# RWKV's keys and receptances projected by blocks: seven products in place of eight

## The chip, the cores and the metric

The kernel runs on one core of one Trainium2 chip. The metric is the device time of one launch in microseconds (us); the profiler's record of one execution gives durations, waits and order. TensorE is PE (its weight loads PEld), VectorE DVE, ScalarE ACT, GpSimdE POOL; SyncE (SP) issues the DMA transfers.

## The reference

One layer over 512 tokens of width 1024, in fp32: a normalization, an input projection, two mixers side by side (a sparse attention, NSA, and RWKV-7), an output projection and an FFN. What the change touches is the projection of RWKV's receptances r and keys k:

```python
proj = rmsnorm(x, ln_mix_g[l]) @ w_in[l]              # (512 x 1024) @ (1024 x 3096)
y_rwkv = rwkv7_mixer(proj[..., NSA_COLS:], ...)
# in rwkv7_mixer:
prev = jnp.pad(cols, ((0, 0), (1, 0), (0, 0)))[:, :-1]
z = cols + (prev - cols) * mu
r, k, v, xw, xa, xg = jnp.split(z, ...)               # 512, 512, 512, 64, 64, 128 columns
kk = k * k_k;  kk = kk * rsqrt(max(sum(kk * kk), 1e-24))
```

## The kernel before

Each fp32 operand of a large product is split into a high part (a cast to fp32r, on ACT) and a low part (the difference, on DVE). A product of two such operands is three matmuls: high by high, high by low, low by high (`mm3`, L331 to 334). Tokens come in four tiles of 128. `norm_T` normalizes a tile, transposes it on PE and leaves its parts in XH and XL, two tensors each for the lower and upper 512 of the 1024 inputs.

The stage `rw_in` (L466) projects five blocks of 256 RWKV features with `feat_cols` (L443). The first holds decay, rate and gate (WA, SG) and runs in two halves of the tokens, since tiles 2 and 3 are normalized while it runs; then two blocks of keys and two of receptances. For a block PE runs over 8 parts of 128 inputs, 2 halves of 128 features and 3 matmuls, 48 in all, of 512 token columns. The weights come in quarters of 128x512, fetched four ahead, split three ahead (`piece`, L428). A block collects in two PSUM banks of one pair (`pa` or `pb`, in turn). When it is done, `shift_mix` (L392) mixes each feature row with the token before: ACT scales the shifted row (`sh`), DVE adds (L398). For the keys ACT squares and PE sums over columns (`pss`, L493); POOL takes a power (`rsk`). WA and SG are such mixes too.

All other streams (values, preparation, scan, attention) wait until `rw_in` sets `rw_kr` (L510). Streams are merged by priority and by a clock of estimated costs (the numbers that each `yield` returns), and a scheduler below that orders each engine's queue; each engine then works its queue in that order. SP's queue carries all loads, and each new load also waits for the one eight before it.

The FFN (L1279 to 1377) already uses seven products: `pair_blocks` for 12 of 16 blocks, `pair_direct` for the first of each half. Its differences of tokens are TT, made in `norms` (L1215 to 1225) in `traw` tiles, its weight sums are `ws`, its products `pw`, the partial sums `wu` and `cc`.

Of the kernel before, what the change touches and what calls it, by code (L numbers as in the profile page):

```python
# [9 lines left out]
F32 = mybir.dt.float32  # L10
# [7 lines left out]
T = 512  # L18
# [5 lines left out]
NT = 4  # L24
RU = 20
RA = 4
# [22 lines left out]
LS = 4  # L49
FV = 10  # L50
UNITS = [(i, g) for g in range(2) for i in range(NT)]
KD = 8
NSA = 1304
RW0 = 1304
# [60 lines left out]
def layer(ctx: ExitStack, tc: tile.TileContext, A, cst, out):  # L115
# [276 lines left out]
    def shift_mix(pa, m, outs):  # L392
# [4 lines left out]
        for i, o_ in enumerate(outs):  # L397
# [6 lines left out]
    COLS.update({f'v{b}': (RW0 + 1024 + 256 * b, 256, True) for b in range(2)})  # L404
    BLOCKS = [(RW0 + 6 * 256, 256, False), (RW0 + 512, 256, False), (RW0 + 768, 256, False), (RW0, 256, False),
              (RW0 + 256, 256, False)] + [COLS[n] for n in ORD]

# [19 lines left out]

    def piece(c0, h):  # L428

        while len(ahead) < 3 and pos_[0] < len(PIECES):  # L430
            p_ = pos_[0]
            c_, n, perm, h_ = PIECES[p_]
            f_ = p_ < 4
            ahead.append((c_, h_, wload(None, 2, n, perm, cycle('zv') if f_ else None, cycle('zr') if f_ else None,
                                        raw_piece(p_), G if f_ and FG else V)))
            for m_ in range(p_ + 1, min(p_ + 1 + RA, RU)):
                raw_piece(m_)
            pos_[0] += 1
        c_, h_, w_ = ahead.pop(0)
        assert (c_, h_) == (c0, h)  # L440
        return w_

    def feat_cols(c0, use, halves=False):  # L443
# [16 lines left out]
        for j in range(2):  # L460
            use(j, pas[j])

    def zt(kind):
        Z[kind] = [at('z' + kind, [128, 4, 128], kind) for _ in range(NT)]

    def rw_in():  # L466
        WA = at('e', [128, T], "WA")
        for n, y_ in enumerate(feat_cols(RW0 + 6 * 256, lambda j, pa: shift_mix(pa, 12 + j, [WA if j == 0 else SG]),
                                         halves=True)):
            load_some(LS)  # L470
            for m_, i in ((N2, 2), (N3, 3)):
                if n == m_:
                    norm_T(i, X[i], g1, XH, XL, 'qq', NPL)
            if n == FV:
                feature_vectors()
            if n == SELN:
                G.tensor_copy(SEL, bc(ident[96:104, 96:104].unsqueeze(2), [8, 8, 64]))
            yield y_
        S.activation(THA[0:64, :], WA[0:64, :], AF.Tanh)
# [16 lines left out]
        for b in range(2):  # L496
            yield from feat_cols(RW0 + (2 + b) * 256, lambda j, pa: use_k(2 * b + j, pa))
        yield 0.0, 0.0
# [4 lines left out]
        for b in range(2):  # L503
            yield from feat_cols(RW0 + b * 256,
                                 lambda j, pa: shift_mix(pa, 2 * b + j, [z_[:, 2 * b + j, :] for z_ in Z['r']]))
        prt = ps([8, NT, 128], "prt")
# [926 lines left out]
```

## Time and profile before

| | |
|---|---|
| median of 3 runs (lowest to highest) | 786.57 us (785.92 to 787.37) |
| profiled execution | 783.81 us |
| its span, first to last instruction | 781.9 us |
| mean granted TensorE clock | 0.987 |
| PE, PEld, DVE, ACT, POOL busy | 97%, 84%, 65%, 51%, 22% of the span |
| DMA | 62.0 MB, mean 79 GB/s |

A matmul's busy time reaches beyond the start of the next, so PE's steps are read from start to start. A row of the timeline with x2 or x4 holds several instructions in a row, and its time is from the first start to the last end. In brackets stands how long the engine was idle before and what ended that. A window's row gives the stretch, its length, the busy time (and instructions) of PE, PEld, DVE, ACT and POOL, the granted TensorE clock (1.00 is 2.4 GHz), the DMA share and GB/s.

### The profile page before, as it was taken

The page shows a single profiled execution, that of the slowest core. Times are in us where ns is not written, and L with a number is a line of the kernel's source. Part 1 is how long each engine was busy: PE and PEld are TensorE (multiplying, and loading weights), DVE is VectorE, ACT ScalarE, POOL GpSimd, SP SyncE. Part 2 cuts the span into 40 slices and gives each one's busy share as a digit, 9 for nine tenths or more (in the row PEclk, how much of TensorE's full clock was granted, in tenths as well). Part 3 has the DMA queues.
Part 4 walks back from the last instruction along what each step waited for, and adds up shares of the span by engine and source line. Part 5 has one row for each costly group of instructions (what it writes and reads, how often), then busy time and mean ns, then how long its engine had stood idle before and what let it go on. Part 6 is the DMA issues. An engine that isn't in the chain of part 4 may idle for free.

```text
span 781.9 us, 18278 instructions
## 1 busy us (share of the span) xinstructions
PE 759.8 (97%) x7357; PEld 657.5 (84%) x7357; DVE 511.8 (65%) x1157; ACT 395.6 (51%) x928; POOL 175.2 (22%) x176
## 2 busy tenths in 40 slices
PE   7999999999989999999999899999999999999998
PEld 5888888889879877887788899998888999978886
DVE  6444385585586789898755888973334989853333
ACT  7343433345444867888544655673332456653330
POOL 5002032240332353434400152300001323100000
PEclk9999999999985999999999999999999999999999
DMA  7741331111000000120343053233323433133212
GB/s 235 206 133 42 94 84 44 44 29 31 15 16 1 29 3 2 30 57 9 114 149 95 17 146 108 69 104 110 96 92 103 118 102 106 62 122 95 95 54 108
DMA packets 67338, 62.00 MB, mean 79 GB/s; under 512 B 6013, under 2 KB 53299, under 8 KB 67254
## 3 DMA queue, kind: packets, MB, share of 16 engines
q1 hardware_dynamic: 67254, 60.83, 25.9%
q8 instruction: 58, 0.95, 0.5%
q14 instruction: 26, 0.21, 0.1%
HBM read 58.72 MB, written 2.10 MB: 78 GB/s over the span
## 4 chain that ended last, share of the span: by engine, by line
PE 84%; DVE 7%; ACT 4%; DMA 3%; issue 1%; SPq 1%; POOL 0%; DVEq 0%; ACTq 0%; POOLq 0%
PE pa L332 8%; PE pa L333 8%; PE pa L334 8%; PE po L332 7%; PE po L333 7%; PE po L334 7%; PE pw L333 5%; PE pw L334 5%; PE pw L332 5%; PE pg L586 2%; PE sc L1075 2%; DMA wraw<-in_w_out_dram 1%; PE py L757 1%; PE pT L1111 1%; PE pz L681 1%
## 5 line engine op out<-in xcount | busy, mean ns | idle before, releaser
L311 ACT CAST whi<-wraw 128x512 fp32r<-128x512 f32 (+1 forms) x128 | 78.7, 622 | 133.4 <-PE po L333 29.1
L312 DVE TENSOR_TENSOR wlo<-wraw,whi 128x512 fp32r<-128x512 f32 (+1 forms) x120 | 86.7, 725 | 86.1 <-ACT whi L311 80.9
L332 PE MATMUL po<-whi 128*128 128x512 f32 x256 | 100.7, 394 | 1.2 <-DVE cc L1361 1.2
L333 PE MATMUL po<-wlo,whi 128*128 128x512 f32 x256 | 101.0, 395 | 0.0
L334 PE MATMUL po<-whi,wlo 128*128 128x512 f32 x256 | 100.7, 393 | 0.0
L333 PE MATMUL pw<-TT,whi 128*128 128x256 f32 x224 | 63.2, 282 | 0.0
L334 PE MATMUL pw<-TT,wlo 128*128 128x256 f32 x224 | 63.0, 281 | 0.0
L332 PE MATMUL pw<-TT,whi 128*128 128x256 f32 x224 | 62.5, 279 | 0.0
L332 PEld LDWEIGHTS po<-whi 128*128 128x128 f32 x256 | 48.0, 188 | 13.0 <-ACT whi L311 1.6
L334 PEld LDWEIGHTS po<-whi,wlo 128*128 128x128 f32 x256 | 48.1, 188 | 11.4
L333 PEld LDWEIGHTS po<-wlo,whi 128*128 128x128 f32 x256 | 48.0, 188 | 11.0
L332 PE MATMUL pa<-XH,whi 128*128 128x512 f32 (+1 forms) x144 | 53.0, 372 | 1.5 <-ACT XH L350 1.5
L333 PE MATMUL pa<-XL,whi 128*128 128x512 f32 (+1 forms) x144 | 53.7, 374 | 0.0
L334 PE MATMUL pa<-XH,wlo 128*128 128x512 f32 (+1 forms) x144 | 52.9, 370 | 0.0
L1291 POOL TENSOR_TENSOR ws<-wq 128x512 f32<-128x512 f32 x14 | 21.5, 1536 | 138.3 <-DMA wq<-in_w_ff_dram 123.2
L311 ACT CAST whi<-ws 128x512 fp32r<-128x512 f32 x56 | 33.0, 617 | 34.7 <-DVE ws L1296 9.5
L312 DVE TENSOR_TENSOR wlo<-ws,whi 128x512 fp32r<-128x512 f32 x56 | 48.2, 870 | 3.1 <-ACT whi L311 3.0
L1089 POOL TENSOR_SCALAR P<-P,z 128x128 f32<-128x128 f32 (+3 forms) x32 | 36.1, 1138 | 60.8 <-DVE z L1038 28.5
L312 DVE TENSOR_TENSOR wlo<-H,whi 128x512 fp32r<-128x512 f32 x32 | 22.1, 690 | 42.1 <-PE po L333 37.4
L334 PE MATMUL pw<-NH,wlo 128*128 128x256 f32 x168 | 47.0, 280 | 0.0
L333 PE MATMUL pw<-NL,whi 128*128 128x256 f32 x168 | 46.8, 279 | 0.0
L332 PE MATMUL pw<-NH,whi 128*128 128x256 f32 x168 | 46.8, 279 | 0.0
(317 smaller groups left out, 2007.9 us busy)
## 6 DMA issues: line engine op xcount, KB each, us to landing
wraw<-in_w_ff_dram SPq DMA_DIRECT2D x72, 256.0 KB
wq<-in_w_ff_dram SPq DMA_DIRECT2D x56, 256.0 KB
wraw<-in_w_in_dram SPq DMA_DIRECT2D x40, 256.0 KB
wraw<-in_w_in_dram SPq DMA_DIRECT2D x8, 268.0 KB
x<-in_x_dram SPq DMA_DIRECT2D x8, 256.0 KB
y<-in_x_dram SPq DMA_DIRECT2D x8, 256.0 KB
wraw<-in_w_out_dram SPq DMA_DIRECT2D x8, 256.0 KB
wraw<-in_w_out_dram SPq DMA_DIRECT2D x16, 128.0 KB
```

The lines of the kernel that those rows point to most:

```text
L311: S.copy(hi, raw)
L312: eng.tensor_tensor(lo, raw, hi.bitcast(F32), op=ALU.subtract)
L332: PE.matmul(o_, l[0], r[0], start=first, stop=False)
L333: PE.matmul(o_, l[0], r[1], start=False, stop=False)
L334: PE.matmul(o_, l[1], r[0], start=False, stop=last)
L586: PE.matmul(pg[:, f], BK[ROW[e], 2 * f + c].rearrange("p a b -> p (a b)"), AR[c][ROW[e], f].rearrange("p a b -> p (a b)"), start=True, sto ...
L681: PE.matmul(o_[rows, b_, :], l[rows, b_, :], r[rows, b_, :], start=True, stop=True)
L757: PE.matmul(py[ROW[a], r, f, :], YL[e][c][:, f, a, :], uv, start=not q and f == 0 and e == 0, stop=True, skip_group_check=True)
L1075: PE.matmul(sc[:, h - h0, :], Qt[:, h, :], KT[br, g, hl].rearrange("p i t -> p (i t)")[:, 0:w], start=hl == 0, stop=hl == 1)
L1089: (G if (h, br) in SCG else V).tensor_scalar(P_[:, h, 0:w], P_[:, h, 0:w], z[:, h:h + 1], None, op0=ALU.mult)
L1111: PE.transpose(pt[:, h, :], P[br][:, h, j * 128:(j + 1) * 128], ident)
L1291: G.tensor_tensor(s3, q[0][0], q[1][0], op=ALU.subtract)
```

## The change

Keys and receptances are projected with `feat_blocks`. With the tokens in two halves (tiles 0 and 1, tiles 2 and 3), the inputs in two halves and the block's features in two halves, the result is a 2x2 product of blocks that is formed from seven products instead of eight. Each is 4 parts of 128 inputs by 3 matmuls of 256 columns. For it four differences of token blocks (`traw`) are made and split into XT, and four sums of weight blocks (`bs`) are made for each block of features, on POOL and DVE. Tiles 2 and 3 keep a raw copy of their transpose (XR, on ACT), tiles 0 and 1 get theirs back as XH + XL on POOL. DVE adds up the products in `wu` and `cc`; the mixes then read `cc`. Weight blocks come as `bq` with `block_load`. The bank of a product alternates between `pa` and `pb`. The values' weights wait until the last parts of the blocks are made (`limit`).

```diff
@@ -22,7 +22,7 @@
 PRI = (1, 2, 2.2, 2.1)
 D = 1024
 NT = 4
-RU = 20
+RU = 4
 RA = 4
 RPL = ('wr', 'uv', 'uv')
 NB = 'aazsaazs'
@@ -48,6 +48,7 @@
 YB = (0.43, 0.4)
 LS = 4
 FV = 10
+BAHEAD = 4
 UNITS = [(i, g) for g in range(2) for i in range(NT)]
 KD = 8
 NSA = 1304
@@ -402,8 +403,7 @@
     COLS = {'cmp': (512, 256, False), 'kv0': (768, 268, False), 'kv1': (1036, 268, False),
             'q0': (0, 256, False), 'q1': (256, 256, False)}
     COLS.update({f'v{b}': (RW0 + 1024 + 256 * b, 256, True) for b in range(2)})
-    BLOCKS = [(RW0 + 6 * 256, 256, False), (RW0 + 512, 256, False), (RW0 + 768, 256, False), (RW0, 256, False),
-              (RW0 + 256, 256, False)] + [COLS[n] for n in ORD]
+    BLOCKS = [(RW0 + 6 * 256, 256, False)] + [COLS[n] for n in ORD]
 
     def turn_of(n):
 
@@ -425,9 +425,10 @@
             nc.sync.dma_start(raws[p_], w_in[:, 2 * h_:2 * h_ + 2, c_:c_ + n])
         return raws[p_]
 
-    def piece(c0, h):
-
-        while len(ahead) < 3 and pos_[0] < len(PIECES):
+    limit = [4]
+
+    def fill():
+        while len(ahead) < 3 and pos_[0] < min(limit[0], len(PIECES)):
             p_ = pos_[0]
             c_, n, perm, h_ = PIECES[p_]
             f_ = p_ < 4
@@ -436,6 +437,10 @@
             for m_ in range(p_ + 1, min(p_ + 1 + RA, RU)):
                 raw_piece(m_)
             pos_[0] += 1
+
+    def piece(c0, h):
+
+        fill()
         c_, h_, w_ = ahead.pop(0)
         assert (c_, h_) == (c0, h)
         return w_
@@ -460,6 +465,112 @@
         for j in range(2):
             use(j, pas[j])
 
+
+    XR = [None] * NT
+    XT = [[], []]
+
+    def x_diffs():
+
+        t_at = cycle(*['kt'] * 8 + ['vh'] * 4 + ['qq'] * 4)
+        for hl in range(2):
+            XT[hl].extend([t_at([128, 2, 256], "XT", F32R) for _ in range(2)] for _ in range(4))
+        for j in range(2):
+            (b11, b21), (b12, b22) = XR[j], XR[j + 2]
+            ts_ = slice(j * 128, j * 128 + 128)
+            T_ = [at('e', [128, 4, 128], "traw") for _ in range(4)]
+            for n, (p_, m_) in enumerate(((b12, b11), (b22, T_[0]), (b22, b12), (b21, T_[1]))):
+                V.tensor_tensor(T_[n], p_, m_, op=ALU.subtract)
+                for kh in range(2):
+                    src = T_[n][:, 2 * kh:2 * kh + 2, :]
+                    hi, lo = (XT[hl][n][kh][:, :, ts_] for hl in range(2))
+                    S.copy(hi, src)
+                    V.tensor_tensor(lo, src, hi.bitcast(F32), op=ALU.subtract)
+                yield
+
+    def xtk(n, k):
+        return XT[0][n][k // 2][:, k % 2, :], XT[1][n][k // 2][:, k % 2, :]
+
+    BC = [RW0 + 512, RW0 + 768, RW0, RW0 + 256]
+    bq_at = cycle('wr', 'wr', 'uv', 'uv', 'uv', 'uv', 'tb', 'bk')
+    bs_at = cycle('ga', 'ga', 'qu', 'lv')
+    bh_at, bl_at = cycle('wh', 'wh', 'wh', 'ar', 'ar'), cycle('wl', 'wl', 'wl', 'ar', 'ar')
+    BQ = {}
+
+    def block_load(n):
+        if n < len(BC) and n not in BQ:
+            BQ[n] = {}
+            for f, h in ((1, 0), (1, 1), (0, 0), (0, 1)):
+                BQ[n][f, h] = bq_at([128, 4, 128], "bq")
+                nc.sync.dma_start(BQ[n][f, h], w_in[:, 4 * h:4 * h + 4, BC[n] + 128 * f:BC[n] + 128 * f + 128])
+
+    def block_parts():
+        sh = [128, 4, 128]
+        for n in range(len(BC)):
+            block_load(n)
+            q = BQ[n]
+            s1, s2, s3, s4 = (bs_at(sh, "bs") for _ in range(4))
+            G.tensor_tensor(s1, q[1, 0], q[1, 1], op=ALU.add)
+            yield split(q[0, 0], sh, bh_at, bl_at)
+            V.tensor_tensor(s2, s1, q[0, 0], op=ALU.subtract)
+            yield split(s2, sh, bh_at, bl_at)
+            G.tensor_tensor(s3, q[0, 0], q[1, 0], op=ALU.subtract)
+            yield split(s3, sh, bh_at, bl_at)
+            yield split(s1, sh, bh_at, bl_at)
+            block_load(n + 1)
+            yield split(q[0, 1], sh, bh_at, bl_at)
+            yield split(q[1, 1], sh, bh_at, bl_at)
+            V.tensor_tensor(s4, q[0, 1], s2, op=ALU.subtract)
+            yield split(s4, sh, bh_at, bl_at)
+
+    parts, pbuf = block_parts(), []
+
+    def more_parts():
+        while len(pbuf) < BAHEAD:
+            w_ = next(parts, None)
+            if w_ is None:
+                if len(pbuf) < 3:
+                    limit[0] = len(PIECES)
+                    fill()
+                return
+            pbuf.append(w_)
+
+    bank4 = cycle_of(pa_, pb_)
+
+    def feat_blocks(use):
+        cc = [at('e', [128, T], "cc") for _ in range(2)]
+        t1, u2, u3, u4 = (at('inv', [128, 256], "wu") for _ in range(4))
+
+        def prod(rhs):
+            p_ = bank4([128, 256], "pw")
+            hi, lo = pbuf.pop(0)
+            more_parts()
+            for k in range(4):
+                r_ = rhs(k)
+                mm3(t4(p_) if len(r_[0].shape) == 3 else p_, (hi[:, k, :], lo[:, k, :]), r_, k == 0, k == 3)
+            return p_
+
+        def plus(o_, *ab):
+            V.tensor_tensor(o_, *ab, op=ALU.add)
+
+        S.copy(t1, prod(lambda k: xk(k, 0, 2)))
+        yield 1.4, 0.0
+        plus(u2, prod(lambda k: xtk(1, k)), t1)
+        yield 1.4, 0.0
+        plus(u3, prod(lambda k: xtk(2, k)), u2)
+        yield 1.4, 0.0
+        p5 = prod(lambda k: xtk(0, k))
+        plus(u4, p5, u2)
+        plus(cc[1][:, 256:512], p5, u3)
+        yield 1.4, 0.0
+        plus(cc[0][:, 0:256], prod(lambda k: xk(4 + k, 0, 2)), t1)
+        yield 1.4, 0.0
+        plus(cc[1][:, 0:256], prod(lambda k: xtk(3, k)), u3)
+        use(1, cc[1])
+        yield 1.4, 0.0
+        plus(cc[0][:, 256:512], prod(lambda k: xk(4 + k, 2, 4)), u4)
+        use(0, cc[0])
+        yield 1.4, 0.0
+
     def zt(kind):
         Z[kind] = [at('z' + kind, [128, 4, 128], kind) for _ in range(NT)]
 
@@ -470,11 +581,25 @@
             load_some(LS)
             for m_, i in ((N2, 2), (N3, 3)):
                 if n == m_:
-                    norm_T(i, X[i], g1, XH, XL, 'qq', NPL)
+                    XR[i] = [at('yl', [128, 4, 128], "xraw") for _ in range(2)]
+                    norm_T(i, X[i], g1, XH, XL, 'qq', NPL, XR[i])
+            if n == 1:
+                for j in range(2):
+                    XR[j] = [at('yl', [128, 4, 128], "xraw") for _ in range(2)]
+                    for b in range(2):
+                        G.tensor_tensor(XR[j][b], XH[b][:, j].bitcast(F32), XL[b][:, j].bitcast(F32), op=ALU.add)
+            if n == 2:
+                block_load(0)
+            if n == 6:
+                xd = x_diffs()
+            if n >= 6:
+                next(xd, None)
             if n == FV:
                 feature_vectors()
             if n == SELN:
                 G.tensor_copy(SEL, bc(ident[96:104, 96:104].unsqueeze(2), [8, 8, 64]))
+            if n == 14:
+                more_parts()
             yield y_
         S.activation(THA[0:64, :], WA[0:64, :], AF.Tanh)
         S.copy(XA[0:64, :], WA[64:128, :])
@@ -494,15 +619,14 @@
 
         zt('k')
         for b in range(2):
-            yield from feat_cols(RW0 + (2 + b) * 256, lambda j, pa: use_k(2 * b + j, pa))
+            yield from feat_blocks(lambda j, pa: use_k(2 * b + j, pa))
         yield 0.0, 0.0
         vss = small(32, "vss")
         V.tensor_scalar(vss, pss.rearrange("p i h -> p (i h)"), 1e-24, None, op0=ALU.max)
         rsk = rsqrt(vss, 32, 'k')
         zt('r')
         for b in range(2):
-            yield from feat_cols(RW0 + b * 256,
-                                 lambda j, pa: shift_mix(pa, 2 * b + j, [z_[:, 2 * b + j, :] for z_ in Z['r']]))
+            yield from feat_blocks(lambda j, pa: shift_mix(pa, 2 * b + j, [z_[:, 2 * b + j, :] for z_ in Z['r']]))
         prt = ps([8, NT, 128], "prt")
         for i in range(NT):
             PE.transpose(prt[:, i, :], rsk[:, 8 * i:8 * i + 8], ident)
```

On DVE, from the last low parts of the normalized tokens (XL) to the two mixes WA and SG, which read the first block's banks. Before:

```order
L353 TENSOR_TENSOR XL<-pt,XH 128x512 x2
L293 COPY VEC<-pvec 128x66
L294 TENSOR_SCALAR OMU<-VEC 128x14
L295 TENSOR_SCALAR KAH<-VEC 128x4
L296 TENSOR_SCALAR KAC<-VEC 128x4
L398 SCALAR_TENSOR_TENSOR WA<-pa,OMU,sh 128x512
L833 SCALAR_TENSOR_TENSOR GK<-gq 128x64 x2
L398 SCALAR_TENSOR_TENSOR SG<-pa,OMU,sh 128x512
```

And the end of the same stretch now, with the tiles' numbers (wlo_465, wlo_470 and wlo_536 are the low parts of the second, third and sixth product's weights, XT_347 to XT_350 low parts of differences, bs_573 a sum for the second key block):

```order
L313 TENSOR_TENSOR wlo_465<-bs_455,whi_464 128x512
L957 SCALAR_TENSOR_TENSOR GK_172<-gq_1901 128x64 x3
L313 TENSOR_TENSOR wlo_470<-bs_456,whi_469 128x512
L313 TENSOR_TENSOR wlo_536<-bq_265,whi_535 128x512
L487 TENSOR_TENSOR XT_347<-traw_401,XT_339 128x2x128
L295 TENSOR_SCALAR OMU_108<-VEC_107 128x14
L487 TENSOR_TENSOR XT_348<-traw_401,XT_340 128x2x128
L487 TENSOR_TENSOR XT_349<-traw_402,XT_341 128x2x128
L487 TENSOR_TENSOR XT_350<-traw_402,XT_342 128x2x128
L514 TENSOR_TENSOR bs_573<-bs_572,bq_513 128x512
L399 SCALAR_TENSOR_TENSOR WA_177<-pa_178,OMU_108,sh_483 128x512
L399 SCALAR_TENSOR_TENSOR SG_165<-pa_179,OMU_108,sh_487 128x512
```

WA and SG moved from behind the vectors of the features to behind all low parts of the differences.

On SP, where the first weights of the blocks (`bq`) are issued now, behind CT and the rows of vectors:

```order
L247 DMA CT<-in_consts_dram 128x580
L247 DMA vrow<-in_rwkv_mu_dram 8x128
L247 DMA vrow<-in_rwkv_mu_dram 2x2x64 x2
L247 DMA vrow<-in_rwkv_mu_dram 2x128
L247 DMA vrow<-in_rwkv_k_k_dram 4x128
L247 DMA vrow<-in_rwkv_k_a_dram 4x128
L247 DMA vrow<-in_rwkv_r_k_dram 4x128
L247 DMA vrow<-in_rwkv_lnx_w_dram 2x2x64 x2
L247 DMA vrow<-in_rwkv_lnx_b_dram 2x2x64 x2
L504 DMA bq<-in_w_in_dram 128x4x128 x3
```

Before, two quarters of the first key block's weights stood ahead of CT, one behind it and one among the vectors.

On PE much later, between the preparation of the last tiles and the first scores, first before, then now:

```order
L797 MATMUL pgt<-SG,G2P 128x128 x4
L702 MATMUL pz<-Tn,QU 32x32 x16
L1053 MATMUL pcs<-KCT,QT 128x32 x4
```

```order
L921 MATMUL pgt<-SG,G2P 128x128 x4
L1177 MATMUL pcs<-KCT,QT 128x32 x4
L826 MATMUL pz<-Tn,QU 32x32 x16
```

The scores of the compressed keys (pcs) moved ahead of a step of the inverse (pz).

## Rows read from the trace of the kernel before

**Rows 1.** The page's chain that ended last, by engine; and one piece of the chain.

```profile
PE 84%; DVE 7%; ACT 4%; DMA 3%; issue 1%; SPq 1%; POOL 0%; DVEq 0%; ACTq 0%; POOLq 0%
...
121.38 1.67 PE ph L871 x14
```

**Rows 2.** Windows, summed over 20 to 74.6 us: busy time by engine.

```profile
sum 54.60, PE 54.60 PEld 46.17 DVE 21.25 ACT 20.98 POOL 6.23; mean PE 10.92 PEld 9.23 DVE 4.25 ACT 4.20 POOL 1.25
```

**Rows 3.** Timeline of PE, a direct block: start, duration, instruction; then key sums.

```profile
39.64 0.39 PE L334 MATMUL pa<-XH,wlo 128*128 128x512 f32 x1
...
43.57 0.40 PE L333 MATMUL pa<-XL,whi 128*128 128x512 f32 x1
...
43.80 1.84 PE L493 MATMUL pss<-CT,sq 128*128 128x2 f32 x16
```

**Rows 4.** Timeline of PE in the FFN's blocks; then its additions, by line.

```profile
500.65 0.28 PE L332 MATMUL pw<-TT,whi 128*128 128x256 f32 x1
...
504.90 0.28 PE L332 MATMUL pw<-NH,whi 128*128 128x256 f32 x1
...
507.83 0.28 PE L332 MATMUL pw<-NH,whi 128*128 128x256 f32 x1
...
510.56 0.28 PE L332 MATMUL pw<-TT,whi 128*128 128x256 f32 x1
...
L1361 DVE TENSOR_TENSOR cc<-pw,wu x56: 407/411/419, 470.3 to 691.9; 128x256 f32<-128x256 f32 x56
```

**Rows 5.** Timeline of DVE where the FFN's differences are made; then their window.

```profile
443.37 0.68 DVE L1219 TENSOR_TENSOR traw<-xraw 128x512 f32<-128x512 f32 x1
443.97 0.75 DVE L1225 TENSOR_TENSOR TT<-traw,TT 128x256 fp32r<-128x256 f32 x2
444.64 0.68 DVE L353 TENSOR_TENSOR NL<-pt,NH 128x512 fp32r<-128x512 f32 x1
...
437.00:452.00 15.00, 12.94 (x97) 11.93 (x96) 14.69 (x31) 10.11 (x26) 2.47 (x2) 1.00 0.21 59
```

**Rows 6.** Timeline of the projection's start and end, several engines.

```profile
20.35 1.28 DVE L353 TENSOR_TENSOR XL<-pt,XH 128x512 fp32r<-128x512 f32 x2
...
27.13 0.39 PE L333 MATMUL pa<-XL,whi 128*128 128x512 f32 x1
...
27.69 0.75 DVE L398 SCALAR_TENSOR_TENSOR WA<-pa,OMU,sh 128x512 f32<-128x512 f32 x1 [3.43 <-ACT sh L395]
...
33.02 0.75 DVE L398 SCALAR_TENSOR_TENSOR SG<-pa,OMU,sh 128x512 f32<-128x512 f32 x1
...
74.31 0.69 ACT L395 ACTIVATE sh<-pa,VEC 128x511 f32<-128x511 f32 x1 [1.66 <-PE pa L334]
```

**Rows 7.** Timeline of SP's issues at the start, and the first reader of x.

```profile
1.13 0.84 SPq L198 DMA_DIRECT2D x<-in_x_dram  x2
...
3.70 0.63 ACT L341 ACTIVATE nt<-x 128x512 f32<-128x512 f32 x1 [1.70 <-DMA x<-in_x_dram]
...
11.56 2.43 SPq L246 DMA_DIRECT2D vrow<-in_rwkv_mu_dram  x4
```

**Rows 8.** Timeline of POOL and DVE side by side; then four mixes of keys.

```profile
14.93 2.55 POOL L312 TENSOR_TENSOR wlo<-wraw,whi 128x512 fp32r<-128x512 f32 x2
...
16.32 1.71 DVE L312 TENSOR_TENSOR wlo<-wraw,whi 128x512 fp32r<-128x512 f32 x1
...
480.35 1.14 DVE L312 TENSOR_TENSOR wlo<-ws,whi 128x512 fp32r<-128x512 f32 x1
...
38.01 1.13 DVE L398 SCALAR_TENSOR_TENSOR k<-pa,OMU,sh 128x128 f32<-128x128 f32 x4 [1.54 <-ACT sh L395]
```

**Rows 9.** Windows around the longest gap of PE, and PE's row behind it.

```profile
226.00:230.00 4.00, 0.89 (x35) 0.67 (x33) 3.92 (x8) 1.59 (x4) 1.89 (x2) 1.00 0.20 67
230.00:250.50 20.50, 20.50 (x163) 19.00 (x164) 12.56 (x66) 10.88 (x48) 5.37 (x5) 0.51 0.01 2
...
229.29 0.69 PE L702 MATMUL pz<-Tn,QU 32*32 32x32 f32 x32 [3.11 <-DVE Tn L694]
```

## The prediction

> **What bounds the kernel now.** I read the page first: its chain that ended last is PE for 84% [rows 1]. Then the windows: from 20 to 74.6 us, the input projection of this change, PE is busy without a break while DVE works 21.25 us and ACT 20.98 us of the 54.6 [rows 2]. Here the time is what PE streams, and DVE has room. The timeline shows what a matmul costs there: busy times overlap, so the step from start to start counts. 512 columns: 39.64 to 43.57 us is 17 steps, 0.231 us each [rows 3]. 256 columns, in the FFN, where seven products already replace eight: 36 steps from 500.65 to 504.90 us, 0.118 each, and 24 from 507.83 to 510.56, 0.114 [rows 4]; I take 0.1175.
>
> **The change on PE.** A direct block of 256 features is 48 matmuls of 512 columns, 48 x 0.231 = 11.1 us. With seven products it is 7 x 12 = 84 of 256 columns, 84 x 0.1175 = 9.87 us. That is 1.23 us a block, 4.9 us over four, and all that the change can take away. The column sums behind the two key blocks (16 records, 1.84 us each [rows 3]) stay.
>
> **The change on DVE.** Removed: 16 low parts of weights. Added: 28 of them, 8 differences of tokens, 16 low parts of 128x256, 8 weight sums, 24 additions of products. With 0.68 us for a 128x512 operation, 0.75/2 for a 128x256 pair and 0.41 for an addition [rows 4, 5]: 28 x 0.68 is 19.0, 16 x 0.68 is 10.9, and in all +8.2 + 5.4 + 6.0 + 5.4 + 9.8 = 34.8 us. With the 21.25 there already it makes 56 us in a stretch of 54.6 that is to become 49.7. Durations overlap a little (0.60 from start to start for 0.68 [rows 5]), some 100 operations by 0.08, so 48 us: DVE goes from half idle to full, and its order now decides.
>
> Its order at the start is what I price. The decay-and-gate block runs direct and holds both banks of one pair until its two mixes (WA and SG) have read them. The seven products alternate between the pairs, so the second, fourth and sixth need a bank of that pair. Before, WA stood four instructions behind the last XL and ran at 27.69 us, as soon as its product was done [rows 6]. Now WA stands behind 42 DVE instructions counted from the blocks' first weight part: by the order 19 of 128x512 (6 low parts, 8 differences, 2 XL, 3 weight sums), 16 of 128x256 and 7 small ones.
>
> - When it starts: DVE and ACT both stop at the first weight part until its transfer lands. It is issued behind CT and ten small vector loads. The first four of those ended at 14 us before [rows 7], seven more at about 0.3 us each bring the second weight quarter to 16.0, and an x load took 1.13 to 3.70 = 2.57 us from issue to its first reader [rows 7]: landed 18.6, cast 0.6, so DVE begins at 19.2. Bounds 18.2 (no wait for slots) and 21.
> - What it does: 19 x 0.60 + 16 x 0.335 (0.67 for two, [rows 5]) + 0.8 for the small ones = 17.6 us.
> - What POOL costs it: POOL now adds up XR (four 128x512) and the weights' sums (four until then). A DVE operation with both inputs in SBUF took 1.71 us in place of 0.68 beside two POOL operations [rows 8], another 1.14 [rows 8]. I take 0.6 for each of six of the eight that overlap, 3.7 us; bounds 0 and 1.27, a POOL operation's whole time, for all eight, 10.2.
>
> The Trainium skill, SBUF — State Buffer, "SBUF: two separate sides", has the pair of ports that VectorE and GpSimd share as an exclusive lock, held for a whole instruction. Rows 8 agree that such operations stretch. By the rule alone each POOL operation could cost its full time, and WA would come 6.5 us later than I say; the trace's second stretch shows less than half of that, so I stay with the rows.
>
> So WA starts at 19.2 + 17.6 + 3.7 = 40.5, done 41.2. On PE the third and fifth products go ahead of the second in the order (they use the other pair), but the third waits for low parts of differences that stand five to nine DVE instructions before WA (about 38). After 41.2 the second, fourth, sixth and seventh products remain: 48 x 0.1175 = 5.6, end 46.8. Before, the block's PE work runs from 27.13 [rows 6] with 46 matmuls left, 46 x 0.231 = 10.6, end 37.8. The first block is therefore 9.0 us late (4.3 with no cost of POOL and the early start, 17.3 with both upper bounds).
>
> Blocks two to four give back 3 x 1.23 = 3.7. A receptance block loads DVE with 9 x 0.60 + 6 x 0.41 + 8 x 1.13/4 [rows 8] + 2 x 0.6 = 11.3 us beside 9.87 on PE, a key block too but beside 9.87 + 1.84. One of the two receptance blocks is held for this, the last one's mixes are behind PE's need: 1.3 us. Sum: 9.0 - 3.7 + 1.3 = 6.6 us late where the last projected block ended, at 74.3 us [rows 6].
>
> At no cost: ACT's 4 raw copies, 16 casts and 12 more weight casts, near 16 us on 20.98 of 54.6 [rows 2]; if DVE kept pace they would be next. The weight loads of the compression now wait for slots of the differences, to about 78 us, while their first matmul is at 121 us [rows 1]; the third value piece stands behind seven of them in SP's queue, 0 to 2 us, I take 0. All else waits for the keys and receptances, so a delay here shifts the whole rest.
>
> The profiled execution took 783.81 us (span 781.9 and 1.9 around it), 2.8 under the median of the runs, 786.57. 783.81 + 6.6 is 790.4; set on the median, 793.2 us.
>
> **Rivals.**
> *The prologue keeps up (PE stays the bound).* For it: the same differences in the FFN took some 14 us of DVE without PE stopping for long (12.94 of 15 us busy) [rows 5]. Against: there two direct blocks cover them, here one half block. With a stall of 0 to 2 us the gain is 3 to 4.9: 782 to 784.
> *The clock falls.* At 226 to 230 us PE worked 0.89 of 4 us, waited 3.11 us for DVE, and then ran 20.5 us at a granted 0.51, the 1.2 GHz level [rows 9]. My sum leaves PE idle 2 us before the low parts of tile 3 (XL stands behind four differences now), 2.5 us before the fifth product's low part, 3.5 before the third, 2 before the second: gaps of that kind. At the lower level 48 to 100 matmuls take twice 0.1175: 5.6 to 11.8 us more, 799 to 805, say 800. Against: the gaps are broken by a dozen matmuls. This case ends slower, and decides from one unbroken gap like the one at 226 us.
> *The cold stretch at 230 us goes away.* The order changes there: four small products (pcs) come ahead of the waiting pz, so the 3.11 us gap is cut. If the clock then stays at 2.4 GHz, the 20.5 us cannot shrink under DVE's 12.56 in them [rows 9], so up to 7.9, say 7: with my 6.6, 786.2. Against: DVE's chain behind pd is the same.
> *The lock costs its full price* is in my range: 6.5 more, 799.7.
>
> The Trainium skill, TensorE: Matmul & The Clock Gate, "What's actually happening", says that the array's clock follows how busy it was lately; rows 9 agree (1.00 before the gap, 0.51 behind it). By it the second and third rivals are real, and would give 800 and 786.2 as worked out.
>
> **How the numbers follow.** A late first block 0.48, with its own range 788 to 799; the clock in the prologue 0.16; the prologue keeps up 0.16; the cold stretch gone 0.20, of which 0.08 ends faster, 0.07 the same, 0.05 slower. A measurement tells about 0.2% (1.6 us) from no change. Slower 0.48 + 0.16 + 0.05, less 0.02 of the first that may end within it: 0.67; same 0.09; faster 0.24. The range 784 to 802 leaves out the better half of the case in which the prologue keeps up, and the far end of the lock's and the clock's.
>
> **What would show it.** WA on DVE near 40 us in place of 27.69; PE idle by 8 to 10 us between 22 and 41 us, ended by DVE; DVE busy over 80% from 20 to 75 us; product steps near 0.1175 in the later blocks; the last mix of the receptances, at 74.31 us before [rows 6], some 6 us later. I am wrong if WA runs before 33 us or PE has no gap there, or if the later stages move by more than the projection does.

## The result and the profile after

The changed kernel takes 794.41 us in the median of three executions beside 786.97: the ratio is 1.0097, with a 95% interval of 1.0072 to 1.0123. A fourth execution ran at a granted clock of 0.555, took 1208.32 us and is left out. So the change makes the kernel slower by 1%. The profiled execution took 795.9 us with a span of 794.1, 12.2 us above that of the profile before. The medians lie only 7.4 us apart: 783.81, the profile before, is below all four runs before, and 795.9 is the longest of the three after.

The chain that ended last, on the page of the profile after, still goes mostly to PE, and DVE's share grows by a point [rows 1]:

```profile
PE 84%; DVE 8%; DMA 3%; ACT 3%; SPq 1%; issue 1%; POOL 0%; DVEq 0%; ACTq 0%; POOLq 0%
```

The windows of the projection, cut at PE's gaps and at the end of each block (columns: stretch and length, busy time and instructions of PE, PEld, DVE, ACT and POOL, granted clock, DMA share, GB/s):

```profile
20.00:28.00 8.00, 4.32 (x37) 4.11 (x35) 7.96 (x7) 4.67 (x12) 7.34 (x6) 0.98 0.81 211
28.00:31.10 3.10, 3.02 (x14) 3.02 (x15) 3.10 (x9) 2.25 (x6) 0.00 (x0) 0.51 0.77 217
31.10:41.20 10.10, 5.96 (x49) 5.56 (x48) 10.10 (x23) 4.97 (x11) 2.90 (x2) 1.00 0.28 67
41.20:48.10 6.90, 6.18 (x26) 5.62 (x27) 6.70 (x14) 3.44 (x6) 2.59 (x5) 0.51 0.32 76
48.10:52.00 3.90, 3.90 (x35) 3.90 (x35) 3.89 (x9) 1.72 (x4) 1.35 (x2) 1.00 0.29 67
52.00:63.60 11.60, 11.60 (x102) 11.60 (x101) 11.41 (x25) 7.76 (x19) 2.56 (x5) 1.00 0.29 69
63.60:75.30 11.70, 11.70 (x103) 11.70 (x101) 11.36 (x26) 8.39 (x19) 3.19 (x4) 1.00 0.09 25
75.30:85.20 9.90, 9.90 (x86) 9.90 (x85) 8.21 (x23) 4.67 (x11) 3.46 (x3) 1.00 0.58 167
sum 65.20, PE 56.58 PEld 55.41 DVE 62.74 ACT 37.85 POOL 23.39; mean PE 7.07 PEld 6.93 DVE 7.84 ACT 4.73 POOL 2.92
```

Before, PE was the full engine and DVE more than half idle [rows 2]. Now DVE works 62.74 of 65.20 us, and PE stands idle for 8.6 us, all of it ahead of the 46th us. The last three windows are the second to fourth block: PE is full in them at a granted 1.00.

DVE's timeline shows how it comes to the mix that frees the first bank (WA). These are the first operations behind the landing of the first weight part, then the mix:

```profile
19.69 1.65 DVE L313 TENSOR_TENSOR wlo<-bq,whi 128x512 fp32r<-128x512 f32 x1 [2.11 <-ACT whi L312]
21.26 1.78 DVE L482 TENSOR_TENSOR traw<-xraw 128x512 f32<-128x512 f32 x1
23.07 1.67 DVE L482 TENSOR_TENSOR traw<-xraw,traw 128x512 f32<-128x512 f32 x1
24.66 1.75 DVE L482 TENSOR_TENSOR traw<-xraw 128x512 f32<-128x512 f32 x1
26.33 1.09 DVE L482 TENSOR_TENSOR traw<-xraw,traw 128x512 f32<-128x512 f32 x1
27.35 0.68 DVE L354 TENSOR_TENSOR XL<-pt,XH 128x512 fp32r<-128x512 f32 x1
...
43.98 0.74 DVE L399 SCALAR_TENSOR_TENSOR WA<-pa,OMU,sh 128x512 f32<-128x512 f32 x1
```

The first five operations stand 1.57, 1.81, 1.59, 1.67 and 1.02 us apart where 0.60 is usual [rows 5]: 4.7 us lost. POOL's timeline beside them:

```profile
17.00 5.48 POOL L590 TENSOR_TENSOR xraw<-XH,XL 128x512 f32<-128x512 f32 x4
22.45 1.74 POOL L516 TENSOR_TENSOR bs<-bq 128x512 f32<-128x512 f32 x1
24.14 1.72 POOL L512 TENSOR_TENSOR bs<-bq 128x512 f32<-128x512 f32 x1
25.92 0.96 POOL L600 COPY THA<-identr 8x512 f32<-8x512 f32 x1
```

POOL's large operations run without a break from 17.0 to 25.9 and a small copy to 26.9, and the stretch of DVE ends with it. PE's timeline has the two long gaps and what the clock does behind the second: eleven matmuls of the third product, then the second product, with 0.21 us from start to start until 47.99 and 0.12 from there.

```profile
28.08 0.58 PE L334 MATMUL pa<-XL,whi 128*128 128x256 f32 x1 [3.76 <-DVE XL L354]
...
41.16 0.48 PE L334 MATMUL pw<-XT,whi 128*128 128x256 f32 x1 [3.90 <-DVE XT L487]
...
44.86 0.55 PE L333 MATMUL pw<-XT,whi 128*128 128x256 f32 x1 [0.47 <-ACT whi L312]
...
47.99 0.35 PE L335 MATMUL pw<-XT,wlo 128*128 128x256 f32 x1
48.18 0.28 PE L333 MATMUL pw<-XT,whi 128*128 128x256 f32 x1
...
52.08 0.28 PE L333 MATMUL pw<-XH,whi 128*128 128x256 f32 x1
...
65.11 0.28 PE L333 MATMUL pw<-XT,whi 128*128 128x256 f32 x1
...
66.88 0.28 PE L333 MATMUL pw<-XT,whi 128*128 128x256 f32 x1
...
85.34 0.60 PE L632 MATMUL prt<-identr,rs_yk 128*8 128x128 f32 x4
```

The second product starts at 44.86. Its last wait, 0.47 us, is put down to ACT's cast of a weight part, which ended at 44.8, 0.1 us behind WA (44.72); in the run with POOL free, further down, the same wait is put down to WA.

At 52.08 the second block begins, so the first ended there (37.8 before). 65.11 to 66.88 is 15 steps, 0.118 each as in the FFN's blocks [rows 4]. The transposes of the key norms (prt) come at 85.34; before, they came at 74.76:

```profile
74.76 0.60 PE L508 MATMUL prt<-identr,rs_yk 128*8 128x128 f32 x4
```

So the projection ends 10.6 us late. ACT's first scaled copy for the last receptance block stood at 74.31 [rows 6], and now:

```profile
84.63 0.72 ACT L396 ACTIVATE sh<-cc,VEC 128x511 f32<-128x511 f32 x1
```

From there the shift passes on nearly unchanged (10.3 to 10.6 us) for some 106 us. The ph matmuls of the chain stood at 121.38 [rows 1] and stand at 132.01 now, and the recurrence's first puu product (a mark used below) moves from 180.39 to 191.00. PE's wait for Tn and the stretch at the lower clock around it [rows 9] are still there; that stretch is even 27.3 us in place of 20.5 in this execution:

```profile
240.45 1.06 PE L826 MATMUL pz<-Tn,QU 32*32 32x32 f32 x32 [2.59 <-DVE Tn L818]
...
239.30:266.60 27.30, 26.15 (x212) 23.21 (x213) 20.15 (x92) 15.91 (x62) 8.54 (x9) 0.50 0.03 11
```

Of the 12.2 us between the two spans 10.6 thus stand at puu. Another 1.5 come behind 450 us, where the FFN begins: PE waits 1.42 us for the low parts NL in both traces (443.50 before, 454.31 now), but now its granted clock falls there, while in the trace before the windows from 443 to 449 us have 1.00:

```profile
454.00:457.00 3.00, 2.69 (x12) 2.69 (x13) 3.00 (x7) 2.90 (x8) 0.00 (x0) 0.55 0.00 0
```

### The profile page after: what moved, and what is told of

It reads as the page before. It is cut to its first block, busy times and chain, and to the rows that moved or that the text cites. A ratio compares the mean times of both kernels' runs of the same rounds, so it can differ in the third digit from the quotient of the medians.

```text
span 794.1 us, 18728 instructions
## 1 busy us (share of the span) xinstructions
PE 766.3 (97%) x7501; PEld 670.9 (84%) x7501; DVE 546.1 (69%) x1229; ACT 412.2 (52%) x964; POOL 195.3 (25%) x188
## 4 chain that ended last, share of the span: by engine, by line
PE 84%; DVE 8%; DMA 3%; ACT 3%; SPq 1%; issue 1%; POOL 0%; DVEq 0%; ACTq 0%; POOLq 0%
PE pw L334 7%; PE pw L333 7%; PE pw L335 7%; PE po L333 7%; PE po L334 7%; PE po L335 7%; PE pa L333 6%; PE pa L334 6%; PE pa L335 6%; PE sc L1199 3%; PE pg L710 3%; PE pT L1235 2%; PE pd L805 1%; PE py L881 1%; PE pz L805 1%; PE pv L1252 1%
## 5 line engine op out<-in xcount | busy, mean ns | idle before, releaser
L312 ACT CAST whi<-wraw 128x512 fp32r<-128x512 f32 (+1 forms) x112 | 68.8, 622 | 122.6 <-PE po L334 30.5
L313 DVE TENSOR_TENSOR wlo<-wraw,whi 128x512 fp32r<-128x512 f32 (+1 forms) x104 | 73.1, 705 | 78.8 <-ACT whi L312 75.7
L333 PEld LDWEIGHTS po<-whi 128*128 128x128 f32 x256 | 48.0, 188 | 12.2 <-ACT whi L312 1.1
L335 PEld LDWEIGHTS po<-whi,wlo 128*128 128x128 f32 x256 | 48.1, 188 | 11.4
L334 PEld LDWEIGHTS po<-wlo,whi 128*128 128x128 f32 x256 | 48.1, 188 | 11.0
L1213 POOL TENSOR_SCALAR P<-P,z 128x128 f32<-128x128 f32 (+3 forms) x32 | 36.6, 1155 | 48.7 <-DVE z L1162 11.5
L333 PEld LDWEIGHTS pw<-TT,whi 128*128 128x128 f32 x224 | 42.2, 189 | 0.0
L334 PEld LDWEIGHTS pw<-TT,whi 128*128 128x128 f32 x224 | 42.1, 188 | 0.0
L335 PEld LDWEIGHTS pw<-TT,wlo 128*128 128x128 f32 x224 | 42.1, 188 | 0.0
```

What stands on the lines that cost most here:

```text
L312: S.copy(hi, raw)
L313: eng.tensor_tensor(lo, raw, hi.bitcast(F32), op=ALU.subtract)
L333: PE.matmul(o_, l[0], r[0], start=first, stop=False)
L334: PE.matmul(o_, l[0], r[1], start=False, stop=False)
L335: PE.matmul(o_, l[1], r[0], start=False, stop=last)
L1213: (G if (h, br) in SCG else V).tensor_scalar(P_[:, h, 0:w], P_[:, h, 0:w], z[:, h:h + 1], None, op0=ALU.mult)
```

## Experiments

The theory: the first block is late by the work that DVE has to do before it, stretched by POOL at the start. The rivals: WA's place in DVE's order (the bank), PE's clock, and a cost in the later stages. Four edits of the changed kernel were to tell them apart; the clock has an edit of its own further down. Ratios are to the kernel before as it ran beside each, with 95% intervals in brackets.

**The first key block direct.** The other three by seven products, the differences beside the direct block.

```diff
-        for b in range(2):
-            yield from feat_blocks(lambda j, pa: use_k(2 * b + j, pa))
+        for n, y_ in enumerate(feat_cols(RW0 + 512, lambda j, pa: use_k(j, pa))):
+            next(xd, None)
+            ...
+        yield from feat_blocks(lambda j, pa: use_k(2 + j, pa))
```

> The first key block is projected directly, as before; the other three by seven products, and the differences of the tokens are made beside the direct block. If what cost the changed kernel its time is DVE's amount of work ahead of the first block (DVE was busy without a break from 19.7 to 47 us), the direct block's 12.9 us of PE now cover it: three blocks gain 3 x 1.23 = 3.7 us, less 0 to 2 us of stall, so 783 to 785 beside 787 of before. If the cost lies elsewhere (receptance blocks that load DVE too much, or later stages that the new loads disturb), it stays slower than before: 789 to 793.

Measured: 1.017 [1.0124, 1.0215], slower than the changed kernel; both expectations missed it. But the trace splits the loss: prt comes at 77.42, 2.7 us late in place of 10.6, and the other 10 us are lost behind 225 us. The direct block covers the second gap, not the first: PE still waits 3.75 us for the tokens' low parts (XL), which stand behind two differences that take 1.75 and 1.64 us beside POOL (at 21.56 and 23.34).

**POOL kept free.** Raw copies on ACT, the weights' sums on DVE.

```diff
-                        G.tensor_tensor(XR[j][b], XH[b][:, j].bitcast(F32), XL[b][:, j].bitcast(F32), op=ALU.add)
...
+        norm_T(i, X[i], g1, XH, XL, 'qq', NPL, XR[i])
...
-            G.tensor_tensor(s1, q[1, 0], q[1, 1], op=ALU.add)
+            V.tensor_tensor(s1, q[1, 0], q[1, 1], op=ALU.add)
```

> The four raw sums of tiles 0 and 1 on POOL are replaced by copies on ACT, and the weights' sums s1 and s3 run on DVE: POOL does no large operation beside DVE in the first 40 us. The theory that DVE operations stood still beside POOL's (1.65 to 1.78 us in place of 0.68): 6.7 us of stretch ahead of WA go and four sums of 0.60 come, WA near 39.7 in place of 43.98, and the whole 4 us shorter than the changed kernel, 791. If the stretch was not from POOL, the four sums only add: 797.

Measured: 1.0206 [1.0173, 1.0239]. The time missed, the place did not. DVE's timeline of this kernel at the start, with the same operations on the same data:

```profile
21.02 0.68 DVE L483 TENSOR_TENSOR traw<-xraw 128x512 f32<-128x512 f32 x1
21.62 0.68 DVE L354 TENSOR_TENSOR XL<-pt,XH 128x512 fp32r<-128x512 f32 x1
22.22 0.68 DVE L313 TENSOR_TENSOR wlo<-bq,whi 128x512 fp32r<-128x512 f32 x1
22.82 0.69 DVE L483 TENSOR_TENSOR traw<-xraw,traw 128x512 f32<-128x512 f32 x1
...
40.31 0.74 DVE L401 SCALAR_TENSOR_TENSOR WA<-pa,OMU,sh 128x512 f32<-128x512 f32 x1
```

Each of these is back at 0.68 or 0.69, WA comes 3.7 us earlier although DVE has four sums more ahead of it, and puu 4.0 earlier (187.03). Again some 11 us are lost later.

**The differences behind the mixes.**

```diff
-            if n >= 6:
-                next(xd, None)
...
+        for _ in x_diffs():
+            pass
         pss = ps([128, NT, 8], "pss")
```

> The differences of the tokens are emitted behind the two mixes (WA and SG), in place of ahead of them. If the cost is WA's place behind 42 DVE instructions (the second product waits for WA's bank), WA comes at 28 to 31 us and much of the 14 us of lateness goes: 785 to 788. If the cost is the amount of DVE work that the first block's products need, whatever the order, WA is early but the second and third products wait for their differences until 43 us or so: 793 to 796.

Measured: 1.029 [1.0255, 1.0326]. WA is early here, and it does not help: PE's timeline shows one wait for the differences in place of several.

```profile
42.74 0.80 PE L333 MATMUL pw<-XT,whi 128*128 128x256 f32 x2 [14.44 <-ACT XT L486]
```

WA stands at 33.39 in place of 43.98, and prt comes at 87.04 in place of 85.34. So WA's place by itself is not the cost; the products wait for the differences instead.

**Without the differences.** The products take the tokens' own parts, so the computation lacks the differences and the raw copies.

```diff
     def xtk(n, k):
-        return XT[0][n][k // 2][:, k % 2, :], XT[1][n][k // 2][:, k % 2, :]
+        return xk(k + 4 * (n % 2), 0, 2)
...
```

> The differences of the tokens and the raw copies that they are made from are left out (the products take the tokens' own parts in their place, so the output is not the reference's): what the seven products and their weights' sums give without the differences. If the differences are the cost, PE is never without work and the whole gain of 4.9 us is there, less the small stall that the weights' parts leave: 782 to 784. If the 28 low parts of weights and the sums already fill DVE, it is 787 to 791.

Measured: 1.0181 [1.0148, 1.0215]. The projection gains 9.0 us by the traces (puu at 182.02), and again 11 us are lost later.

So all four are slower than the changed kernel, with projections that end before its own in three of them. What they share is that the scheduler of the program, which orders the instructions by its own model, had interleaved the recurrence and the attention anew: by the traces some 1,100 to 1,200 of the 7,000 matmuls behind the projection stand elsewhere in PE's order than before in each, though no line there was edited; so do some 900 in the changed kernel, and there it costs nothing. From puu to the last transposes of the FFN's norm (pt) it is 259.5 us before and 259.6 in the changed kernel, but 269.5, 269.7, 268.4 and 271.0 in these four. In the first of them the attention's last transpose pct comes at 380.60 with the recurrence's last product py at 375.51; before, the order was the other way, and the recurrence as early:

```profile
380.60 0.33 PE L1219 MATMUL pct<-identr,pcm 128*128 128x128 f32 x1 [0.53 <-DVE tl L1243]
...
375.51 1.15 PE L884 MATMUL py<-UV,YL 128*64 128x64 f32 x32
```

(the kernel before, the same two rows)

```profile
368.21 0.27 PE L1092 MATMUL pct<-identr,pcm 128*128 128x128 f32 x1
...
374.97 1.15 PE L757 MATMUL py<-UV,YL 128*64 128x64 f32 x32
```

**The late order held.** To take this out, a routine chains the last 5,184 matmuls, 977 instructions of DVE, 742 of ACT and 152 of POOL, which are the same in all these kernels, in the order that the kernel before has them (order alone, no wait is added). By the traces none of the 7,000 stands elsewhere then.

```diff
         layer(tc, args, cst, out)
+        pin_late(tc, nc)      # for each engine: tc.add_manual_dep(eng[k], last.name, NoSync)
```

> The changed kernel, with its instructions behind the projection pinned to the order that the kernel before has there (the order of the first 75 us is the changed kernel's own). The projection ends 10.6 us late as in the changed kernel's profile. If the late order of the changed kernel is worth nothing against that of before, the whole is 787.0 + 10.6 = 797.6, within 2 us; if it gains the 2 to 3 us by which the changed kernel's median stays under that, this one is 797 to 800; if it loses them, 792 to 794.

Measured: 797.75 us beside 787.83, 1.0133 [1.0115, 1.015]; puu at 191.19. The projection's 10.6 us pass to the end. By the medians the changed kernel with its own late order loses 2.5 us less than this one (7.4 and 9.9), but that its order earns them is not shown: the two intervals overlap, the runs were on two chips, and in the traces it is 259.6 us from puu to pt in both.

The same with the first key block direct; for the order to hold, the value block has to take the other pair of banks:

```diff
     def rw_v():
+        turn[0] ^= 1
         zt('v')
```

> The kernel with its first key block direct again (it ended 12 us slower than before though its projection was only 2.7 us late), now with the instructions behind the projection pinned to the order of the kernel before. If the other 10 us came from another order in the recurrence and the attention, they go, and 787.0 + 2.7 = 789.7 stays (788 to 792). If they come from something that the seven products leave behind (memory slots, transfers), it stays near 799.

Measured: 1.0074 [1.0056, 1.0092], 792.75 us. From puu to pt it is 260.4 in place of 269.5, so the 9 us were the order. The 2 us beyond the projection's 2.7 come from the other pair of banks, since the value block now waits there for the last receptance block:

```profile
80.52 0.50 PE L333 MATMUL pa<-XH,whi 128*128 128x512 f32 x1 [1.86 <-DVE cc L553]
```

**The two DVE terms again, with the late order held** (the edits are those above, with the routine added).

> The changed kernel without the large POOL operations in the first 75 us (raw copies on ACT, weights' sums on DVE), now with the late order pinned to that of the kernel before. Its projection ended 4.0 us earlier than the changed kernel's; pinned, the changed kernel took 797.75, so if POOL's stretch of DVE passes to the end in full: 793.7 (793 to 794.5). If only the late order made the difference, 797 to 798.

> The changed kernel with the differences of the tokens and the raw copies left out (output not the reference's), now with the late order pinned to that of the kernel before. Its projection ended 9.0 us earlier than the changed kernel's; if the differences' work on DVE is the cost and passes to the end: 797.75 - 9.0 = 788.8 (788 to 790), still not under the kernel before, because the weights' parts and the banks hold PE too. If nothing but the differences held it, 783.

Measured, on a chip where the kernel before took 785.20: 791.27, 1.0074 [1.0055, 1.0094], and 786.58, 1.0013 [0.9999, 1.0027]. Against the 1.0133 of the changed kernel with the same late order that is 0.6% and 1.2%, 4.6 and 9.4 us. Both pass to the end as their projections said. The two terms overlap, since POOL's raw sums go with the differences. Without any differences the kernel is still not under the one before: PE waits 1.3 us for WA and 1.0 for the squares of the keys, its transposes of the last tile (pt) already stand at 19.32 in place of 17.79, and the weights' parts stay.

**PE kept busy in its gaps.** 42 matmuls whose result nobody reads, in the second gap and ahead of the second product (the first gap stays).

```diff
+            idle = pi_([128, 256], "idle")
+            for _ in range(42):
+                PE.matmul(idle, rows_[4][:, 0, :], xtk(0, 0)[0], start=True, stop=True)
...
```

> The changed kernel, late order pinned to that of before, with 42 throwaway matmuls of 256 columns into an unused bank in PE's gaps of the first block (34 behind the fifth product, 8 ahead of the second), so that PE is not idle there. If PE's clock (0.5 from 41.3 to 48.1 us) costs only what runs behind WA, the first block ends 1.5 us earlier than in the changed kernel (52.0 us there), and the whole is 1 to 2 us under the same kernel without the throwaway matmuls. If the clock's whole 10.2 us at half speed are lost, it is 5 us. If DVE alone sets the end, nothing.

Measured: 795.76, 1.0113 [1.0093, 1.0134], 1.6 us under the same kernel without them, with intervals that overlap. The window that ran at 0.51 now has the full clock:

```profile
41.20:48.10 6.90, 5.99 (x48) 5.60 (x47) 6.90 (x14) 3.56 (x7) 2.59 (x5) 1.00 0.32 76
```

Yet prt moves only from 85.55 to 84.73: the second product still starts at 44.91 behind WA (44.02), and of the 1.4 us that its full clock saves (PE reaches the seventh product at 49.3 in place of 50.7) 0.6 are given back in a wait for a weight's part. So the clock behind the second gap makes 0.8 of the projection's 10.6 us. What it costs behind the first gap (28.0 to 31.1 us) was not run; PE waits 3.90 us for DVE afterwards, so that it costs nothing there is argued, not shown.

**Enough cover.** Both key blocks direct, the two receptance blocks by seven products, the differences emitted from the end of the decay-and-gate block on.

```diff
-            if n >= 6:
+            if n >= 16:
                 next(xd, None)
...
+            for n, y_ in enumerate(feat_cols(RW0 + 512 + 256 * b, lambda j, pa: use_k(2 * b + j, pa))):
+                if b == 0:
+                    next(xd, None)
```

> Both key blocks direct, only the two receptance blocks by seven products, and the differences emitted behind the decay-and-gate block; late order pinned to that of the kernel before. If DVE's amount of work in the first blocks is the cost, two direct blocks (24 us of PE) cover it and 2 x 1.23 = 2.5 us are gained: 784.5 (783.5 to 786). If the blocks by themselves load DVE too much (weights' parts ahead of the first product), 788 to 790.

Measured: 787.2 beside 787.83, 0.9997 [0.9985, 1.0008], above both the 784.5 expected and its range. The cover works (PE has no gap up to 55 us), but one wait for a bank that the keys' mixes still hold remains:

```profile
56.73 0.35 PE L333 MATMUL pw<-XT,whi 128*128 128x256 f32 x1 [1.62 <-DVE k L399]
```

**Three idle banks for the products.**

```diff
-    bank4 = cycle_of(pa_, pb_)
+    bank4 = cycle_of(pa_, pz_, pa_, pq_, pi_, pb_, pb_)
```

> Both key blocks direct and two receptance blocks by seven products, late order pinned, as in the run that came out level with the kernel before; now the products' banks take in three that stand empty during the projection, so that no product waits for a bank that the second key block's mixes still read (PE waited 1.62 us for them, and its products then stood in smaller gaps). If that wait is what is missing from the 2.5 us, 1 to 2 us go: 785 to 786.2 beside 787.2. If DVE's load behind it sets the end, the products only wait elsewhere: 787.

Measured: 783.46 beside 785.20, 0.9987 [0.997, 1.0004]. The wait is gone (from 20 to 77 us PE waits 0.2 us in all), and prt comes at 74.43, 0.3 us ahead of before. It is the best of these versions and the only one not behind before in its projection; that it is faster is not settled, since the interval holds 1. Of the 2.5 us that two blocks save, 1.1 were gone before the first of them: WA stands at 28.83 in place of 27.69.

The marks of all runs, in us of their profiles, and the ratios:

| kernel | WA | prt | puu | puu to pt | ratio |
|---|---|---|---|---|---|
| before | 27.69 | 74.76 | 180.39 | 259.5 | 1 |
| changed | 43.98 | 85.34 | 191.00 | 259.6 | 1.0097 |
| first key block direct | 33.41 | 77.42 | 183.05 | 269.5 | 1.017 |
| POOL free | 40.31 | 79.96 | 187.03 | 269.7 | 1.0206 |
| differences late | 33.39 | 87.04 | 192.81 | 268.4 | 1.029 |
| no differences | 32.22 | 76.39 | 182.02 | 271.0 | 1.0181 |
| changed, order held | 44.01 | 85.55 | 191.19 | 259.6 | 1.0133 |
| first direct, order held | 33.35 | 77.36 | 185.08 | 260.4 | 1.0074 |
| POOL free, order held | 39.99 | 79.94 | 186.98 | 260.3 | 1.0074 |
| no differences, order held | 31.64 | 75.33 | 180.95 | 260.3 | 1.0013 |
| gaps filled, order held | 44.02 | 84.73 | 190.38 | 259.4 | 1.0113 |
| keys direct, order held | 30.13 | 76.76 | 182.44 | 259.2 | 0.9997 |
| and idle banks | 28.83 | 74.43 | 180.10 | 259.7 | 0.9987 |

## Why the prediction was right, and where its sizes were off

The sign, the mechanism and the time (793.2 for 794.41) came out; the projection's own lateness did not: 10.6 us for 6.6. The first block ends 5.3 us later than forecast (52.08 for 46.8), 3.5 of them at WA and 1.6 in the matmuls behind it, and the 1.3 us for the receptance blocks did not come.

- *What PE gains.* 1.23 us a block. From the first block's end to prt it is 33.26 us after (52.08 to 85.34) and 36.96 before (37.8 to 74.76): 3.7 for three blocks, as forecast.
- *DVE goes from half idle to full.* It does, and the runs without differences show that their work, with what POOL adds to it, is 9 to 10 us of the lateness. The sum has an addition missing in each block: the kernel makes 28 (seven a block), not 24, 1.6 us more on DVE.
- *When DVE starts.* 19.2 forecast, 19.69 measured.
- *WA at 40.5.* It came at 43.98. With the 17.6 us of work the rest of the 24.3 is 6.7 us of stretch (4.7 in the five operations above, 1.0 and 1.1 at 35.65 and 41.03 beside two later sums), in place of the 3.7 that I took from [rows 8] and inside its bounds of 0 and 10.2. This is the step that failed, a size: six of POOL's eight large operations met DVE, as I had counted, but each cost it about 1.1 us and not 0.6. The two later sums beside the operations that they meet, some of which lose nothing:

```profile
34.79 1.95 POOL L512 TENSOR_TENSOR bs<-bq 128x512 f32<-128x512 f32 x1 [7.35 <-DVE wlo L313]
40.25 2.03 POOL L516 TENSOR_TENSOR bs<-bq 128x512 f32<-128x512 f32 x1 [3.52 <-DVE wlo L313]
...
35.18 0.41 DVE L487 TENSOR_TENSOR XT<-traw,XT 128x256 fp32r<-128x256 f32 x1
35.65 1.37 DVE L487 TENSOR_TENSOR XT<-traw,XT 128x256 fp32r<-128x256 f32 x1
41.03 1.28 DVE L295 TENSOR_SCALAR OMU<-VEC 128x14 f32<-128x14 f32 x1
```

The price stood in the trace before. Of the operations that stretch beside POOL in its FFN, my row at 480.35 (1.14 us) is one of the mildest; most take 1.34 to 1.82, as these two do:

```profile
461.58 1.52 DVE L1289 TENSOR_TENSOR ws<-ws,wq 128x512 f32<-128x512 f32 x1
468.38 1.66 DVE L312 TENSOR_TENSOR wlo<-ws,whi 128x512 fp32r<-128x512 f32 x1
```

The Trainium skill's page SBUF — State Buffer, "SBUF: two separate sides", has the shared pair held for a whole instruction, for DVE operations with two inputs in SBUF among others. I had set that rule aside for the milder row at 480.35. The run with POOL free shows that POOL's operations make the stretch, 1.65 to 1.78 us falling to 0.68. The rule's full price is not what the rows show, though: by it WA would have come at 47.0, 3 us too late. Two of POOL's four raw sums (17.0 to 19.7) ran before DVE had begun and cost nothing, and the operation at 35.18 takes its usual 0.41 us inside POOL's row of 34.79 to 36.74.
- *The 48 matmuls behind WA.* 5.6 us forecast, 7.2 measured (44.86 to 52.08), since their first 3.1 us ran at the lower clock. The rival of the falling clock thus happened in part, at a price of 0.8 us by the run with filled gaps and not the 5.6 to 11.8 I gave it: most of the time at the lower clock lay where PE had to wait for DVE anyway. PE's gaps were 3.76, 0.24, 3.90, 0.25 and 0.47 us, 8.6 in all, for 10 forecast.
- *1.3 us for DVE's load in the receptance blocks.* Not seen: PE has no wait from 50.6 to 85.34, with DVE at 8.21 of 9.90 us in the last block.
- *The rest only shifts.* True in the traces up to 225 us, and with the late order held to the end. But the runs show only 7.4 us (7.6 by the ratio) of the projection's 10.6. So the good agreement of the time rests in part on luck, on two errors of opposite sign: 4.0 us too little in the projection, and nothing for the 3 us or so by which the runs stay under it. Where these 3 us come from is open: the 10.6 are read from one execution of each kernel, and the late order changed too, but the trace shows no gain from it. I had looked at the new order at one place only (the wait for Tn), where the forecast that the stretch might stay away was wrong.
- *The prologue keeps up.* It does not: even with the differences taken out, the projection ends 0.6 us late. Only with both key blocks direct and three more banks does it.

## What to carry to other kernels

A product saved on the bound engine is worth its time only where the engine that prepares it has the room at that moment. Here the room existed on average (DVE more than half idle over the projection before), but the differences fall due at the first block, and only as many direct blocks as cover them would make the saving free. And where a program is ordered by a scheduler's model, an edit's effect has to be read at marks inside the trace, or with the order of the rest held: an untouched stage moved by 9 to 11.5 us here.

## What the runs showed of the hardware that was not expected

PE's first matmuls do not have the same step in executions of the same instructions. In the changed kernel the first matmuls of the decay block run 0.21 us apart until 17.4 us; in the kernel with filled gaps, which is the same up to there, the same matmuls have their 0.12 from the first. The step of 0.21 is that of 41 to 48 us, where the granted clock is 0.51, but the windows at the start give 1.00 in both, so that it is the clock here too is likely and not shown.

```profile
16.62 0.41 PE L333 MATMUL pa<-XH,whi 128*128 128x256 f32 x1
16.84 0.41 PE L334 MATMUL pa<-XL,whi 128*128 128x256 f32 x1
```

(the kernel with filled gaps)

```profile
14.62 0.28 PE L334 MATMUL pa<-XL,whi 128*128 128x256 f32 x1
14.74 0.28 PE L335 MATMUL pa<-XH,wlo 128*128 128x256 f32 x1
```

It makes 1 to 2 us at the start, which matter where PE is the bound there (the run with both key blocks direct began so) and are lost in DVE's work where it is not.

The stretch at the lower clock near 240 us lasted 20.5 or 23.9 us in the runs with the late order held and 20.5 to 27.3 in the others, and came with a gap as small as 2.59 us. A gap of 1.42 us at the start of the FFN is followed by a fallen clock in some executions and not in others, and it is worth about 2 us: from pt to the end of the span it is 343.5 to 344.4 us in the five traces where the clock falls there (the changed kernel with its own and with the held order, the first key block direct with both, the differences late) and 341.9 to 342.7 in the other eight. The 42 throwaway matmuls show the other side, that PE's clock can be held through a wait by work that nobody reads: 1.00 in place of 0.51 from 41.2 to 48.1 us.
